# Attention of a two-layer trunk on one core: both heads of a pair in one operation for small blocks, fillers accumulated in the scores' PSUM banks, a shorter scale chain and another order of fillers

## The chip, the cores and the metric

The kernel runs on one core of a Trainium2 chip. The metric is device time in microseconds, as the median of several executions. Five engines run side by side, each through its own instructions in order: PE multiplies matrices (its weight loads are listed as PEld), DVE and ACT work element by element, POOL does small jobs and some DMA issues, SP issues the weight DMAs. Matrix products end in PSUM, which has eight banks of 128 x 512 float32 here; ACT and DVE carry results from there to on-chip memory.

## The reference

One sequence of 512 tokens of width 1024 goes through two layers. Layer 0 is attention and a gated MLP, layer 1 a gated short convolution and another MLP. All is float32. The attention has 8 forgetting heads (softmax) and 8 stick-breaking heads; cut to what matters here:

```python
q_fox = rms_norm(q[:, :H_FOX], fox_q_g)          # the same for k, and for the stick-breaking heads
logits = einsum('bhqd,bhkd->bhqk', qi, k) * scale + fi[..., :, None] - cum_f[:, :, None, :]
p = softmax(where(causal, logits, -inf));  o_fox = p @ v

z = einsum('bhqd,bhkd->bhqk', qi, k) * scale                     # stick breaking
log_one_minus = where(strict, log_sigmoid(-z), 0.0)
later = cumsum(log_one_minus, reverse=True) - log_one_minus
w = where(strict, exp(log_sigmoid(z) + later), 0.0);  o_sb = w @ v
out = concatenate([o_fox, o_sb]) @ w_out
```

## The kernel before

Every large product is done as three matmuls on a high and a low part of each operand (`mm3`, lines 248 to 250, and `mm3_rhs`, 503 to 505), to keep float32 accuracy. Weights come by DMA in tiles `raw` and are split by ACT (line 227, `whi`) and DVE (line 228, `wlo`).

The attention works on pairs of heads p = 0 to 7 (0 to 3 forgetting, 4 to 7 stick-breaking) and query blocks b = 0 to 3 of 128 rows; a block (p, b) has n = 128(b+1) keys. For a block, `logits` puts the scores of the two heads e = 0, 1 into two PSUM banks, and ACT and DVE turn them into weights `w`: maximum, exponential, reciprocal and scaling for forgetting heads; two sigmoids, a backward scan (line 639) and a product (line 640) for the others. `turn` transposes `w` on PE into a bank `psc` and splits the result into `pt` (ACT line 662, DVE line 663). `weigh` multiplies two blocks' `pt` with the values into a bank `psa`, and ACT and DVE (lines 688, 689) read it out as `o`.

Between those steps PE gets other work, "fillers": generators that yield after each step of a product. `queries_keys(p)` makes the queries and keys of a pair, with their sums of squares (`sums`, line 539), a transpose of these (`turned_sums`, 547), a reciprocal root on DVE (`scales`, lines 549 to 568) and transposes of the widened scale (`rows`, line 575); `values(g)` makes the values of two pairs; `output(0)` is the first half of the output projection. `fill(us)` spends a quota of filler work by a running clock of estimated PE time, `after(us, fn)` puts a function on that clock. The constants at the head set those quotas and delays: `PRE` is the filler work ahead of the first block, `ROWS` the delay from the scale chain to the transposes of `rows`.

PSUM is dealt out by `bank(tag)`: two banks "a" (queries, keys, values, `weigh`, output), four banks "b" (scores) and two banks "c" (all transposes and small sums). The program is written in this order, but a scheduler then sets each engine's order, by its own costs and by which slots are free; the excerpts of that order below show the result. Names there carry numbers: `psa168_2985` is one allocation of a bank "a", `w420` the weights of pair 4, block 2, head 0, `qk_hi60` the high part of the queries of pair 6, and a bracket tells which engines' semaphores the instruction waits for.

Of the kernel before, what the change touches and what calls it, by code (L numbers as in the profile page):

```python
# [25 lines left out]
P = 128  # L26
S = 512
# [23 lines left out]
def trunk(  # L51
# [207 lines left out]
    class Norm:  # L259
# [23 lines left out]
                dve.tensor_tensor(self.acc, self.acc, sq, op=ALU.add)  # L283

        def scale(self, sums):
            v = tiny.tile([P, NB], F32, tag="nv", name=f"nv_{self.name}")
# [195 lines left out]
    def values(g):  # L482
        ws = [weights(), weights(AHEAD - 1)]
        v = v_tiles[g] = ap_.tile([P, NB, 4, 2, HD], F32R, tag="v", name=f"v{g}", bufs=2)
        n = 256 if g else 264
        for b in range(NB):
            acc = bank("a")
            tok = slice(b * P, (b + 1) * P)
            for k in range(ND):
                w = ws[k // 4]  # L490
                mm3_rhs(acc[:, 0:n], (hs_hi[:, k, tok], hs_lo[:, k, tok]), (w[0][:, k % 4, :], w[1][:, k % 4, :]), k == 0, k == ND - 1)
                spend(0.33)
                yield 1
# [3 lines left out]
            dve.scalar_tensor_tensor(v[:, b, :, 1, :], src, r, f32(v[:, b, :, 0, :]), op0=ALU.mult, op1=ALU.subtract)  # L497
# [6 lines left out]
        pe.matmul(acc, lhs[0], w[1], start=False, stop=False)  # L504
        pe.matmul(acc, lhs[1], w[0], start=False, stop=last)  # L505

    rx2 = const.tile([P, NB], F32, tag="rx2", name="rx2")

    def square_norm():
        dve.tensor_tensor(rx2, norm.col, norm.col, op=ALU.mult)  # L510
        dve.tensor_scalar(rx2, rx2, 1.0 / HD, None, op0=ALU.mult)

    halves, q_scale, done = {}, {}, set()

# [5 lines left out]
    def queries_keys(p):  # L520


        fox = p < 4
        v = tiny.tile([P, NB, 2, 2], F32, tag="qv", name=f"qv{p}")
        r = tiny.tile([P, NB, 2, 2], F32, tag="qr", name=f"qr{p}")
        kept, got, sqs = {}, {}, []
        halves[p] = got

# [16 lines left out]
        def turned_sums(t, flat):  # L545
            for i in range(2):
                pe.transpose(t[:, (2 + i) * P:(3 + i) * P], flat[:, i * P:(i + 1) * P], ident)
            spend(0.25)
            dve.tensor_tensor(
                v, t[:, 2 * P:4 * P].rearrange("p (i b c) -> p b i c", i=2, b=NB)[:, :, :, 0:2],  # L550
                rx2[:, :, None, None].to_broadcast([P, NB, 2, 2]), op=ALU.mult,
            )
            scales()

        def scales():
            vf, rf = (t.rearrange("p b i h -> p (b i h)") for t in (v, r))
            dve.tensor_scalar(vf, vf, EPS, None, op0=ALU.add)
            rsqrt(rf, vf, 16, f"qk{p}")
            rf = r.rearrange("p b i h -> p b (i h)")
            dve.tensor_tensor(rf, rf, norm.col[:, :, None].to_broadcast([P, NB, 4]), op=ALU.mult)  # L560
            if not fox:
                s = q_scale[p] = aw.tile([P, 2, NB, 2], F32, tag="qscale", name=f"qscale{p}", bufs=3)
                dve.tensor_copy(s[:, 0], r[:, :, 1, :])
                dve.tensor_scalar(s[:, 1], r[:, :, 1, :], -1.0, None, op0=ALU.mult)
            wides = {}
            for i in kept:
                wides[i] = work.tile([P, S], F32, tag="u0", name=f"qwide{p}{i}").rearrange("p (b h d) -> p b h d", b=NB, h=2)
                dve.tensor_copy(wides[i], r[:, :, i, :][:, :, :, None].to_broadcast([P, NB, 2, HD]))
            after(ROWS, lambda: rows(wides))

        def rows(wides):
# [7 lines left out]
            done.add(("qk", p))  # L579

        for i in range(2):
            acc = bank("a")
            yield from products(acc, weights())
            sq = work.tile([P, S], F32, tag="sq", name=f"sq_{p}{i}")
            act.activation(sq, acc, AF.Square)
# [7 lines left out]
                act.activation(kept[i], acc, AF.Copy, scale=g)  # L593
            sqs.append(sq)
        after(SUMS, sums)

    def logits(p, b):

# [19 lines left out]
        ws = []  # L618
        for e in range(2):
            s = ss[e]  # L620
            w = aw.tile([P, S], F32, tag="w", name=f"w{p}{b}{e}", bufs=WB)
            ws.append(w)
            if fox:
                top = tiny.tile([P, 1], F32, tag="top", name=f"top{p}{b}{e}")
                dve.reduce_max(top, s[:, 0:n], axis=AX.X, negate=True)
                total = tiny.tile([P, 1], F32, tag="total", name=f"total{p}{b}{e}")
                act.activation(w[:, 0:n], s[:, 0:n], AF.Exp, bias=top, accum_out=total)
                inv = tiny.tile([P, 1], F32, tag="inv", name=f"inv{p}{b}{e}")
                dve.reciprocal(inv, total)
                dve.tensor_scalar(w[:, 0:n], w[:, 0:n], inv, None, op0=ALU.mult)  # L630
            else:
                scale = q_scale[p]
                rest = aw.tile([P, S], F32, tag="rest", name=f"rest{p}{b}{e}")
                act.activation(rest[:, 0:n], s[:, 0:n], AF.Sigmoid, scale=scale[:, 1, b, e:e + 1])
                act.activation(w[:, 0:n - 1], s[:, 0:n - 1], AF.Sigmoid, scale=scale[:, 0, b, e:e + 1])

                pool.memset(w[:, n - 1:n], 0.0)
                back = rest[:, 1:n][:, ::-1]
                dve.tensor_tensor_scan(back, back, begin[:, S - n + 1:S][:, ::-1], 0.0, op0=ALU.mult, op1=ALU.max)  # L639
                dve.tensor_tensor(w[:, 0:n - 1], w[:, 0:n - 1], rest[:, 1:n], op=ALU.mult)  # L640
        return ws

    pts = {}

    def turn(p, b, ws):

        half, n = b // 2, (b + 1) * P
        if b % 2 == 0:
            pts[p, half] = []
            for e in range(2):  # L650
                both = [aw.tile([P, NB, 256], F32R, tag=f"pt{i}", name=f"pt{p}{half}{e}{i}", bufs=PT) for i in range(2)]
                for t in both:
                    pool.memset(f32(t[:, 2 * half + 1, 0:P]), 0.0)
                pts[p, half].append(both)
        at_ = slice((b % 2) * P, (b % 2 + 1) * P)
        for e in range(2):
            t = bank("c")
            for k in range(b + 1):
                pe.transpose(t[:, k * P:(k + 1) * P], ws[e][:, k * P:(k + 1) * P], ident)  # L659
            src = t[:, 0:n].rearrange("p (k q) -> p k q", q=P)  # L660
            hi, lo = pts[p, half][e]
            act.activation(hi[:, 0:b + 1, at_], src, AF.Copy)
            dve.tensor_tensor(lo[:, 0:b + 1, at_], src, f32(hi[:, 0:b + 1, at_]), op=ALU.subtract)
        spend(0.22 * (b + 1))

    def weigh(p, half):
# [5 lines left out]
        to = slice(half * 256, (half + 1) * 256)  # L672
        last = 2 * half + 1
        for e in range(2):
            hi, lo = pts[p, half][e]
            for k in range(last + 1):
                w = v[:, k, 2 * (p % 2) + e].rearrange("p i d -> p (i d)")
                pe.matmul(acc[:, e * 256:(e + 1) * 256], w, hi[:, k, :], start=k == 0, stop=False)
                pe.matmul(acc[:, e * 256:(e + 1) * 256], w, lo[:, k, :], start=False, stop=k == last)
# [131 lines left out]
    after(NORM0, lambda: (norm.scale(sums0), square_norm()))  # L811
    for k in range(ND):
        next(qk0)
    flush()
# [1 line left out]
    attn = ExitStack()  # L816
    ap_ = attn.enter_context(tc.tile_pool(name="attn", bufs=1))
    aw = attn.enter_context(tc.tile_pool(name="aw", bufs=2))

# [9 lines left out]
    run(values(0))  # L829
    log_gate()  # L830
    load_gains()
    for g, ps_ in enumerate(((1, 2), (3, 4), (5, 6), (7,))):
        fillers.extend(queries_keys(p) for p in ps_)
        if g < 3:
            fillers.append(values(g + 1))
# [177 lines left out]
```

## Time and profile before

| what | before |
| --- | --- |
| median of 3 runs | 1221.25 us (1220.8 to 1221.3) |
| profiled execution | 1220.77 us, span 1219.0 us |
| PE busy | 1204.0 us, 99% of the span, 5841 instructions |
| DVE busy | 762.8 us, 63% |
| ACT busy | 503.4 us, 41% |
| POOL busy | 26.6 us, 2% |
| mean busy share of the DMA engines, 40 to 260 us | 0.20 |

The span runs from the first to the last instruction; the profiled execution is 1.8 us longer than its span. The attention lies between about 23 and 260 us of the span; ahead of it are the first norm and products, behind it the output projection's end, the MLPs and the convolution.

### The profile page before, as it was taken

The page shows a single profiled execution, that of the slowest core. Times are in us where ns is not written, and L with a number is a line of the kernel's source. Part 1 is how long each engine was busy: PE and PEld are TensorE (multiplying, and loading weights), DVE is VectorE, ACT ScalarE, POOL GpSimd, SP SyncE. Part 2 cuts the span into 40 slices and gives each one's busy share as a digit, 9 for nine tenths or more (in the row PEclk, how much of TensorE's full clock was granted, in tenths as well). Part 3 has the DMA queues.
Part 4 walks back from the last instruction along what each step waited for, and adds up shares of the span by engine and source line. Part 5 has one row for each costly group of instructions (what it writes and reads, how often), then busy time and mean ns, then how long its engine had stood idle before and what let it go on. Part 6 is the DMA issues. An engine that isn't in the chain of part 4 may idle for free.

```text
span 1219.0 us, 15006 instructions
## 1 busy us (share of the span) xinstructions
PE 1204.0 (99%) x5841; PEld 973.4 (80%) x5841; DVE 762.8 (63%) x1250; ACT 503.4 (41%) x787; POOL 26.6 (2%) x139
## 2 busy tenths in 40 slices
PE   8999999999999999999999999999999999999998
PEld 7887877778888888888888888888888888888886
DVE  5887888887867777663333555465776767672222
ACT  6556576655544443432222222233434344442120
POOL 4000000000000000000000000000000000000000
PEclk9999999999999999999999999999999999999999
DMA  7312121213233333323333333323233332322330
GB/s 196 88 36 70 36 69 36 70 62 96 87 102 89 97 93 94 96 81 93 94 95 104 89 102 87 104 87 104 87 93 98 89 102 87 103 87 88 121 102 35
DMA packets 182696, 108.14 MB, mean 89 GB/s; under 512 B 4732, under 2 KB 175020, under 8 KB 182624
## 3 DMA queue, kind: packets, MB, share of 16 engines
q1 hardware_dynamic: 182080, 106.94, 29.7%
q8 instruction: 46, 0.75, 0.3%
q0 software_dynamic: 384, 0.17, 0.1%
q14 instruction: 26, 0.21, 0.1%
q10 hardware_dynamic: 160, 0.07, 0.0%
HBM read 105.06 MB, written 2.10 MB: 88 GB/s over the span
## 4 chain that ended last, share of the span: by engine, by line
PE 91%; DVE 6%; ACT 2%; issue 1%; DMA 0%; SPq 0%; DVEq 0%; POOL 0%; ACTq 0%
PE psa L248 13%; PE psa L250 12%; PE psa L249 12%; PE psb L248 12%; PE psb L250 12%; PE psb L249 12%; PE psa L503 2%; PE psa L504 2%; PE psa L505 2%; PE psb L504 2%; PE psb L503 2%; PE psb L505 2%; DVE rest L639 1%; PE psc L659 1%; PE psb L610 1%
## 5 line engine op out<-in xcount | busy, mean ns | idle before, releaser
L227 ACT ACTIVATE whi<-raw 128x1024 fp32r<-128x1024 f32 (+3 forms) x199 | 208.9, 1050 | 362.7 <-PE psb L249 134.9
L228 DVE TENSOR_TENSOR wlo<-raw,whi 128x1024 fp32r<-128x1024 f32 (+3 forms) x199 | 240.4, 1209 | 160.2 <-ACT whi L227 159.1
L248 PE MATMUL psa<-hs_hi,whi 128*128 128x512 f32 x544 | 219.4, 403 | 2.5 <-DVE o L689 1.3
L250 PE MATMUL psa<-hs_hi,wlo 128*128 128x512 f32 x544 | 215.1, 395 | 0.2 <-DVE wlo L228 0.2
L249 PE MATMUL psa<-hs_lo,whi 128*128 128x512 f32 x544 | 214.6, 395 | 0.0
L248 PE MATMUL psb<-hs_hi,whi 128*128 128x512 f32 x480 | 189.9, 396 | 0.0
L250 PE MATMUL psb<-hs_hi,wlo 128*128 128x512 f32 x480 | 189.8, 395 | 0.0
L249 PE MATMUL psb<-hs_lo,whi 128*128 128x512 f32 x480 | 188.7, 393 | 0.0
L347 DVE SCALAR_TENSOR_TENSOR u<-y,taps,u 128x510 f32<-128x510 f32 (+1 forms) x176 | 131.1, 748 | 3.3 <-ACT u L344 0.4
L248 PEld LDWEIGHTS psa<-hs_hi,whi 128*128 128x128 f32 x544 | 102.3, 188 | 25.7 <-issue 2.3
L250 PEld LDWEIGHTS psa<-hs_hi,wlo 128*128 128x128 f32 x544 | 102.2, 188 | 25.0 <-DVE wlo L228 1.1
L249 PEld LDWEIGHTS psa<-hs_lo,whi 128*128 128x128 f32 x544 | 102.3, 188 | 22.2 <-DVE hs_lo L758 0.4
L249 PEld LDWEIGHTS psb<-hs_lo,whi 128*128 128x128 f32 x480 | 90.1, 188 | 21.4
L250 PEld LDWEIGHTS psb<-hs_hi,wlo 128*128 128x128 f32 x480 | 90.1, 188 | 21.4
L248 PEld LDWEIGHTS psb<-hs_hi,whi 128*128 128x128 f32 x480 | 90.3, 188 | 20.2
L885 DVE TENSOR_TENSOR y<-psb,nrow_n 128x512 f32<-128x512 f32 x44 | 30.4, 691 | 83.3 <-PE psb L250 83.3
L339 ACT ACTIVATE a<-u 128x512 fp32r<-128x512 f32 x44 | 27.9, 634 | 118.7 <-DVE u L890 118.7
L889 ACT ACTIVATE u<-u 128x512 f32<-128x512 f32 x44 | 27.9, 633 | 91.3 <-DVE u L347 91.3
L344 ACT ACTIVATE u<-y,taps 128x512 f32<-128x512 f32 x88 | 63.1, 719 | 1.2 <-DVE y L885 1.1
L340 DVE TENSOR_TENSOR a<-u,a 128x512 fp32r<-128x512 f32 x44 | 30.5, 692 | 29.4 <-ACT a L339 29.4
L503 PE MATMUL psa<-whi,hs_hi 128*128 128x256 f32 (+1 forms) x128 | 38.3, 299 | 0.8 <-ACT qk L593 0.7
L505 PE MATMUL psa<-whi,hs_lo 128*128 128x256 f32 (+1 forms) x128 | 36.3, 283 | 0.0
(251 smaller groups left out, 1818.3 us busy)
## 6 DMA issues: line engine op xcount, KB each, us to landing
raw<-in_ffn_w_up SPq DMA_DIRECT2D x88, 512.0 KB, 3.8
raw<-in_ffn_w_down SPq DMA_DIRECT2D x30, 512.0 KB, 3.7
raw<-in_attn_w_in SPq DMA_DIRECT2D x24, 512.0 KB, 4.0
raw<-in_conv_w_in SPq DMA_DIRECT2D x24, 512.0 KB, 3.8
raw<-in_ffn_w_down SPq DMA_DIRECT2D x16, 448.0 KB, 3.6
raw<-in_attn_w_out SPq DMA_DIRECT2D x8, 512.0 KB, 3.5
raw<-in_conv_w_out SPq DMA_DIRECT2D x8, 512.0 KB, 3.9
x_tok<-in_x SPq DMA_DIRECT2D x4, 512.0 KB, 6.5
```

The source lines that it names most:

```text
L227: return (act.activation(hi[:, at_], raw[:, at_], AF.Copy), dve.tensor_tensor(lo[:, at_], raw[:, at_], f32(hi[:, at_]), op=ALU.subtract))
L228: dve.tensor_tensor(lo[:, at_], raw[:, at_], f32(hi[:, at_]), op=ALU.subtract))
L248: made = [pe.matmul(acc, w[0], rhs[0], start=first, stop=False), pe.matmul(acc, w[0], rhs[1], start=False, stop=False), pe.matmul(acc, w[1 ...
L249: pe.matmul(acc, w[0], rhs[1], start=False, stop=False),
L250: pe.matmul(acc, w[1], rhs[0], start=False, stop=last)]
L340: dve.tensor_tensor(lo, src, f32(hi), op=ALU.subtract)
L344: act.activation(dst, src, AF.Copy, scale=tap(2))
L347: dve.scalar_tensor_tensor(dst[:, d:], src[:, 0:S - d], tap(j), dst[:, d:], op0=ALU.mult, op1=ALU.add)
L503: pe.matmul(acc, lhs[0], w[0], start=first, stop=False)
L504: pe.matmul(acc, lhs[0], w[1], start=False, stop=False)
L505: pe.matmul(acc, lhs[1], w[0], start=False, stop=last)
L885: dve.tensor_tensor(y, acc, norm.row, op=ALU.mult)
```

## The change

- In `logits` and `turn`, blocks with b < 2 are done for both heads at once (`at_once`): one reciprocal, one product with the scanned row, one PSUM bank of transposes and one split into `pt`, where two stood before. Blocks with b = 2, 3 keep one operation per head. `w` and `pt` become one tile for both heads, with the same total of buffers.
- The scanned row `rest` is one tile for the whole attention, placed at its right end, with a column of zeros behind it; the memsets of the last column of `w` on POOL go.
- `queries_keys` for p >= 1 and `values` for g >= 1 accumulate in banks "b" in place of "a".
- The scale chain: `least`, made once, and one operation on DVE (scale and add) stand for a product, an addition and a later product with `ncol` for each pair.
- Fillers run in the order 1, 2, v1, 3, 4, 5, v2, 6, 7, v3 in place of 1, 2, v1, 3, 4, v2, 5, 6, v3, 7. `PRE` goes from 12 to 14, `ROWS` from 5 to 8.

```diff
-PRE = 12.0
+PRE = 14.0
-SUMS, FLAT, ROWS = 3.0, 1.5, 5.0
+SUMS, FLAT, ROWS = 3.0, 1.5, 8.0
...
-    for g, ps_ in enumerate(((1, 2), (3, 4), (5, 6), (7,))):
+    for g, ps_ in enumerate(((1, 2), (3, 4, 5), (6, 7), ())):
...
     def values(g):
...
-            acc = bank("a")
+            acc = bank("b" if g >= 1 else "a")
...
-            dve.tensor_tensor(
-                v, t[:, 2 * P:4 * P].rearrange("p (i b c) -> p b i c", i=2, b=NB)[:, :, :, 0:2],
-                rx2[:, :, None, None].to_broadcast([P, NB, 2, 2]), op=ALU.mult,
+            dve.scalar_tensor_tensor(
+                v.rearrange("p i b h -> p (i b) h"), t[:, 2 * P:4 * P].rearrange("p (j c) -> p j c", c=32)[:, :, 0:2],
+                1.0 / HD, least[:, :, None].to_broadcast([P, 2 * NB, 2]), op0=ALU.mult, op1=ALU.add,
             )
...
-            dve.tensor_scalar(vf, vf, EPS, None, op0=ALU.add)
             rsqrt(rf, vf, 16, f"qk{p}")
-            dve.tensor_tensor(rf, rf, norm.col[:, :, None].to_broadcast([P, NB, 4]), op=ALU.mult)
...
-            acc = bank("a")          # in queries_keys
+            acc = bank("b" if p >= 1 else "a")
...
+    def at_once(b):
+        return (slice(0, 2),) if b < 2 else (slice(0, 1), slice(1, 2))
...
+            for es in at_once(b):
+                for e in range(es.start, es.stop):
+                    act.activation(rest[:, e, keys], ss[e][:, 0:n], AF.Sigmoid, scale=scale[:, 1, b, e:e + 1])
+                    act.activation(w[:, e, :], ss[e][:, 0:n], AF.Sigmoid, scale=scale[:, 0, b, e:e + 1])
+                    back = rest[:, e, keys][:, ::-1]
+                    dve.tensor_tensor_scan(back, back, begin[:, keys][:, ::-1], 0.0, op0=ALU.mult, op1=ALU.max)
+                dve.tensor_tensor(w[:, es], w[:, es], rest[:, es, S - n + 1:S + 1], op=ALU.mult)
...
-        for e in range(2):
-            t = bank("c")
-            for k in range(b + 1):
-                pe.transpose(t[:, k * P:(k + 1) * P], ws[e][:, k * P:(k + 1) * P], ident)
-            src = t[:, 0:n].rearrange("p (k q) -> p k q", q=P)
-            hi, lo = pts[p, half][e]
-            act.activation(hi[:, 0:b + 1, at_], src, AF.Copy)
-            dve.tensor_tensor(lo[:, 0:b + 1, at_], src, f32(hi[:, 0:b + 1, at_]), op=ALU.subtract)
+        for es in at_once(b):
+            t = bank("c")[:, 0:(es.stop - es.start) * n].rearrange("p (e k q) -> p e k q", k=b + 1, q=P)
+            for e in range(es.start, es.stop):
+                for k in range(b + 1):
+                    pe.transpose(t[:, e - es.start, k, :], w[:, e, k * P:(k + 1) * P], ident)
+            act.activation(hi[:, es], t, AF.Copy)
+            dve.tensor_tensor(lo[:, es], t, f32(hi[:, es]), op=ALU.subtract)
```

What stands where moves on every engine. On PE, where the scores of block (6, 0) are made (`psb` with queries `qk_hi60`), and a filler's product begins in a bank "a" in their midst; before:

```order
L610 MATMUL psb169_3004<-qk_hi60_2889,qk_hi61_2657 128x256 [waits Activation_49]
L248 MATMUL psa168_2985<-hs_hi_111,whi22_2662 128x512 [waits DVE_49,PE_49]
L249 MATMUL psa168_2985<-hs_lo_112,whi22_2662 128x512
L250 MATMUL psa168_2985<-hs_hi_111,wlo22_2663 128x512
L248 MATMUL psa168_2985<-hs_hi_111,whi22_2662 128x512
L249 MATMUL psa168_2985<-hs_lo_112,whi22_2662 128x512
L250 MATMUL psa168_2985<-hs_hi_111,wlo22_2663 128x512
L610 MATMUL psb170_3005<-qk_hi60_2889,qk_hi61_2657 128x256
L610 MATMUL psb169_3004<-qk_lo60_2890,qk_hi61_2657 128x256
```

The same block after; the filler is now `values(3)`, already under way in a bank "b", and the transposes of `w53` stand between the scores' first and later parts:

```order
L504 MATMUL psb154_2737<-wlo23_2629,hs_hi_111 128x256
L612 MATMUL psb155_2750<-qk_hi60_2714,qk_hi61_2477 128x256 [waits Activation_49]
L612 MATMUL psb156_2751<-qk_hi60_2714,qk_hi61_2477 128x256
L505 MATMUL psb154_2737<-whi23_2628,hs_lo_112 128x256
L657 MATMUL psc157_2775<-ident_84,w53_2663 128x128 [waits DVE_49]
L657 MATMUL psc157_2775<-ident_84,w53_2663 128x128 x3
L657 MATMUL psc158_2782<-ident_84,w53_2663 128x128 [waits DVE_49]
L657 MATMUL psc158_2782<-ident_84,w53_2663 128x128 x3
L612 MATMUL psb155_2750<-qk_lo60_2715,qk_hi61_2477 128x256 [waits DVE_49]
```

The first filler matmul no longer asks for a bank "a"; the scores themselves still wait for the queries that ACT and DVE split.

On PE, the transposes of block (4, 2), whose first head goes to one bank "c" and whose second to the other; before, the sums of pair 5 (`flat5`) hold a bank too:

```order
L659 MATMUL psc140_2516<-ident_84,w420_2397 128x128 x2
L547 MATMUL psc138_2479<-ident_84,flat5_2488 128x128 [waits Activation_49]
L547 MATMUL psc138_2479<-ident_84,flat5_2488 128x128
L248 MATMUL psa135_2438<-hs_hi_111,whi18_2236 128x512
L249 MATMUL psa135_2438<-hs_lo_112,whi18_2236 128x512
L250 MATMUL psa135_2438<-hs_hi_111,wlo18_2237 128x512
L248 MATMUL psa135_2438<-hs_hi_111,whi18_2236 128x512
L249 MATMUL psa135_2438<-hs_lo_112,whi18_2236 128x512
L250 MATMUL psa135_2438<-hs_hi_111,wlo18_2237 128x512
L659 MATMUL psc141_2522<-ident_84,w421_2404 128x128 [waits DVE_49]
```

and after:

```order
L675 MATMUL psa131_2390<-pt401_2271,v2_1999 128x256
L657 MATMUL psc132_2412<-ident_84,w42_2322 128x128 x3
L657 MATMUL psc133_2418<-ident_84,w42_2322 128x128 [waits PE_49]
L657 MATMUL psc133_2418<-ident_84,w42_2322 128x128 x2
L248 MATMUL psb130_2380<-hs_hi_111,whi19_2300 128x512
```

The pair's sums have moved to another place, and the second head's transposes follow the first's without a wait for DVE.

On DVE, the blocks (4, 0) and (4, 1); before, scan and product are four operations for a block, and the split of the transposes two:

```order
L639 SCALAR_TENSOR_TENSOR rest410_2310<-rest410_2310,begin_89 128x255 [waits Activation_49]
L663 TENSOR_TENSOR pt3111_2197<-psc124_2282,pt3110_2196 128x4x128 [waits Activation_49]
L640 TENSOR_TENSOR w410_2309<-w410_2309,rest410_2310 128x255 [waits DVE_49,Activation_49]
L228 TENSOR_TENSOR wlo19_2330<-raw19_2328,whi19_2329 128x1024 [waits DMAHW2_49,PE_49,Activation_49]
L639 SCALAR_TENSOR_TENSOR rest411_2317<-rest411_2317,begin_89 128x255 [waits Activation_49]
L640 TENSOR_TENSOR w411_2316<-w411_2316,rest411_2317 128x255 [waits DVE_49,Activation_49]
L663 TENSOR_TENSOR pt4001_2362<-psc129_2369,pt4000_2361 128x128 [waits PE_49,Activation_49,Pool_49]
L663 TENSOR_TENSOR pt4011_2366<-psc130_2373,pt4010_2365 128x128 [waits PE_49,Activation_49,Pool_49]
```

and after:

```order
L639 SCALAR_TENSOR_TENSOR rest_357<-rest_357,begin_89 128x256 [waits Activation_49] x2
L640 TENSOR_TENSOR w41_2212<-w41_2212,rest_357 128x2x256 [waits DVE_49,Activation_49]
L497 SCALAR_TENSOR_TENSOR v2_1999<-psb117_2182,ncol_n0_324,v2_1999 128x4x64 [waits Activation_49]
L575 TENSOR_TENSOR qn50_2257<-qk50_1912,psc122_2252 128x512 [waits PE_49]
L685 TENSOR_TENSOR o31_2263<-psa121_2235,o31_2263 64x256 [waits Activation_49]
L659 TENSOR_TENSOR pt401_2271<-psc123_2274,pt400_2270 128x2x128 [waits Activation_49,Pool_49]
```

The product and the split stand once for both heads.

More of the change, by code (lines that the diff above doesn't have):

```diff
@@ L285, in scale @@
         def scale(self, sums):
[L286 removed]
+            v = self.mean = tiny.tile([P, NB], F32, tag="nv", name=f"nv_{self.name}")
             dve.tensor_scalar(v, sums, 1.0 / D, EPS, op0=ALU.mult, op1=ALU.add)
@@ L505, in mm3_rhs, with least_square @@
         pe.matmul(acc, lhs[1], w[0], start=False, stop=last)
[L507 to L511, printed above, removed]
+    least = const.tile([P, 2 * NB], F32, tag="least", name="least")
+    def least_square():
+        for i in range(2):
+            dve.tensor_scalar(least[:, i * NB:(i + 1) * NB], norm.mean, EPS, None, op0=ALU.mult)
     halves, q_scale, done = {}, {}, set()
@@ L523, in queries_keys @@
         fox = p < 4
-        v = tiny.tile([P, NB, 2, 2], F32, tag="qv", name=f"qv{p}")
-        r = tiny.tile([P, NB, 2, 2], F32, tag="qr", name=f"qr{p}")
+        v = tiny.tile([P, 2, NB, 2], F32, tag="qv", name=f"qv{p}")
+        r = tiny.tile([P, 2, NB, 2], F32, tag="qr", name=f"qr{p}")
         kept, got, sqs = {}, {}, []
@@ L617, in logits @@
         spend((4 if fox else 3) * wide * 0.00044 + (0.12 if fox else 0))
-        ws = []
-        for e in range(2):
[L620 to L640, printed above, removed]
@@ L641, in logits @@
-        return ws
+        w = aw.tile([P, 2, S], F32, tag="w", name=f"w{p}{b}", bufs=2)[:, :, 0:n]
+        if fox:
+            top, total, inv = (tiny.tile([P, 2], F32, tag=t, name=f"{t}{p}{b}") for t in ("top", "total", "inv"))
+            for e in range(2):
+                dve.reduce_max(top[:, e:e + 1], ss[e][:, 0:n], axis=AX.X, negate=True)
+                act.activation(w[:, e, :], ss[e][:, 0:n], AF.Exp, bias=top[:, e:e + 1], accum_out=total[:, e:e + 1])
+            for es in at_once(b):
+                dve.reciprocal(inv[:, es], total[:, es])
+                for e in range(es.start, es.stop):
+                    dve.tensor_scalar(w[:, e, :], w[:, e, :], inv[:, e:e + 1], None, op0=ALU.mult)
+        else:
+            scale = q_scale[p]
+            keys = slice(S - n, S)
+            for es in at_once(b):
[5 more added lines that the diff above has]
+                dve.tensor_tensor(w[:, es], w[:, es], rest[:, es, S - n + 1:S + 1], op=ALU.mult)
@@ L674, in weigh @@
         for e in range(2):
-            hi, lo = pts[p, half][e]
+            hi, lo = (t[:, e] for t in pts[p, half])
             for k in range(last + 1):
@@ L810, in trunk @@
         after(b + 0.5, lambda b=b: squares(b))
-    after(NORM0, lambda: (norm.scale(sums0), square_norm()))
+    after(NORM0, lambda: (norm.scale(sums0), least_square()))
     for k in range(ND):
@@ L818, in trunk @@
     aw = attn.enter_context(tc.tile_pool(name="aw", bufs=2))
+    rest = aw.tile([P, 2, S + 1], F32, tag="rest", name="rest", bufs=1)
+    pool.memset(rest[:, :, S:S + 1], 0.0)
     o_tiles = {0: mixed(0)}
@@ L831, in trunk @@
     load_gains()
-    for g, ps_ in enumerate(((1, 2), (3, 4), (5, 6), (7,))):
+    for g, ps_ in enumerate(((1, 2), (3, 4, 5), (6, 7), ())):
         fillers.extend(queries_keys(p) for p in ps_)
```

26 lines of the change are left out of this document (12 added, 14 removed).

## The prediction

> **What bounds the kernel.** I read the page first, then the busy time by stretch, then the list of who waited for whom on PE.
>
> ```profile
> span 1219.0 us, 15006 instructions
> ...
> PE 1204.0 (99%) x5841; PEld 973.4 (80%) x5841; DVE 762.8 (63%) x1250; ACT 503.4 (41%) x787; POOL 26.6 (2%) x139
> ```
>
> PE is busy all but 15.0 us of the span. By stretch (after the length come PE, PEld, DVE, ACT and POOL busy, the granted clock and the DMA share):
>
> ```profile
> 0.00:23.00 23.00, 20.12 (x124) 15.77 (x124) 13.28 (x20) 17.02 (x28) 12.24 (x46) 1.00 0.73 206
> 23.00:40.00 17.00, 16.59 (x133) 15.35 (x131) 12.58 (x51) 8.64 (x16) 0.53 (x1) 1.00 0.37 99
> 40.00:260.00 220.00, 212.10 (x1426) 169.68 (x1425) 181.69 (x461) 136.68 (x310) 13.05 (x88) 1.00 0.20 59
> 260.00:1219.00 959.00, 955.20 (x4165) 772.57 (x4163) 555.30 (x721) 341.11 (x436) 0.76 (x5) 1.00 0.31 93
> ```
>
> The change touches the stretch from 40 to 260. There PE sits idle 220.00 - 212.10 = 7.9 us, at clock 1.00, with DMA at 0.20, and DVE is busy 83% of it. So the ceiling is low: this is a change for those 7.9 us and little else. PE's waits (total, times, longest):
>
> ```profile
> PE psc L659 <- DVE pt L663: 1.7, 2, 1.4
> PE psa L248 <- DVE o L689: 1.6, 2, 1.3
> PE psc L575 <- DVE pt L663: 1.4, 2, 0.9
> PE psa L248 <- DVE h L727: 1.3, 1, 1.3
> ...
> PE psa L503 <- ACT qk L593: 0.7, 2, 0.4
> PE psc L539 <- ACT sq L585: 0.5, 1, 0.5
> ...
> PE psc L575 <- DVE qwide L568: 0.5, 1, 0.5
> PE psc L539 <- DVE pt L663: 0.3, 1, 0.3
> ...
> PE psa L678 <- DVE v L497: 0.2, 1, 0.2
> ```
>
> Most wait for a bank: `psc` until DVE has split an older transpose into `pt`, or `psa` until `o` or `qk` is read out. Not one is for `w` (the softmax or the scan) or for a score bank `psb`. Two places, in time (start, length):
>
> ```profile
> 178.36 0.40 PE L249 MATMUL psa<-hs_lo,whi 128*128 128x512 f32 x1
> 178.59 0.39 PE L250 MATMUL psa<-hs_hi,wlo 128*128 128x512 f32 x1
> 180.36 0.55 PE L659 MATMUL psc<-ident,w 128*128 128x128 f32 x3 [1.38 <-DVE pt L663]
> ```
>
> and on DVE at that time:
>
> ```profile
> 176.90 0.69 DVE L640 TENSOR_TENSOR w<-w,rest 128x511 f32<-128x511 f32 x1
> 177.51 1.22 DVE L639 TENSOR_TENSOR_SCAN rest<-rest,begin 128x511 f32<-128x511 f32 x1
> 178.82 0.69 DVE L640 TENSOR_TENSOR w<-w,rest 128x511 f32<-128x511 f32 x1
> 179.43 0.41 DVE L689 TENSOR_TENSOR o<-psa,o 64x256 f32<-64x256 f32 x1
> 179.77 0.54 DVE L663 TENSOR_TENSOR pt<-psc,pt 128x384 fp32r<-128x384 f32 x1
> ```
>
> This is the wait of `w421` in the order above. The split of the first head's transposes stands on DVE behind a scan, a product and `o`, and ends at 180.31; PE starts at 180.36. Two matmuls start 0.23 us apart but count as busy for 0.39, so each listed wait hides 0.16 us more: this one costs 180.36 - 178.82 = 1.54, not 1.38.
>
> ```profile
> 211.00 0.38 PE L610 MATMUL psb<-qk_hi,qk_hi 64*128 64x256 f32 x1
> 212.69 0.47 PE L248 MATMUL psa<-hs_hi,whi 128*128 128x512 f32 x1 [1.32 <-DVE o L689]
> ```
>
> This is `psa168` of the order: a new filler product needs a bank "a" that `weigh` has just filled and DVE not yet read.
>
> **The change, part by part.** PE has as many instructions after as before, 5833 in the order; nothing is taken from PE but waits and turns.
>
> Banks "a". Fillers for p, g >= 1 leave them, so the wait at 212.69 (1.3) goes, and the smaller of the two `qk` waits (0.7 - 0.4 = 0.3; the other is at the first pair, which stays in "a"). With 0.16 each: -1.9 us. The waits for `h` (1.3) and for `o` at the output projection (0.3) stay; that filler is still in "a".
>
> Banks "c". Five waits, 1.7 + 1.4 + 0.3 = 3.4, with the hidden part 4.2. I laid PE's order end to end (0.23 us for 512 columns, in proportion below, 0.12 for a transpose: an estimate) and counted the allocations that follow within 3.0 us of PE time on the last write of the tile that must come free; the split at 179.77 came free 3 us after its transposes. In "c" there were 24 of these in the attention and are 11, since small blocks take one bank instead of two. I take the waits in proportion, 11/24 kept: -2.3. Ends: 0, if the 11 are the ones that bite, and -4.2.
>
> `rows`. Three more units of `ROWS` put the widened scale's transposes behind the scale chain: the 0.5 (0.7 in full) for `qwide` goes. -0.7; ends 0 and -0.7.
>
> Turns of PE. Scores use half the rows of the array. The order holds them in 38 unbroken runs before and in 34 after (the first excerpt is one of the broken ones).
>
> ```profile
> 205.26 0.28 PE L505 MATMUL psa<-whi,hs_lo 128*128 128x256 f32 x1
> 205.47 0.50 PE L610 MATMUL psb<-qk_hi,qk_hi 64*128 64x512 f32 x2
> ...
> 206.36 0.39 PE L503 MATMUL psa<-whi,hs_hi 128*128 128x256 f32 x1
> ```
>
> From 205.26 to 206.36 is 1.10 us; a 256-wide matmul and three pairs of 512 take 0.12 + 3 x 0.23 = 0.81 without turns. So entering and leaving costs 0.28 us, and four runs fewer -1.1; ends 0 and -1.6.
>
> DVE. Sixteen splits of 128 columns become eight of 256, sixteen of 256 eight of 512, and the scale chain loses two operations of eight pairs:
>
> ```profile
> L663 DVE TENSOR_TENSOR pt<-psc,pt 128x512 fp32r<-128x512 f32 x16 | 10.6, 686 | 1.4 <-ACT pt L662 1.3
> ...
> L663 DVE TENSOR_TENSOR pt<-psc,pt 128x256 fp32r<-128x256 f32 x16 | 6.3, 416 | 0.9 <-ACT pt L662 0.8
> ...
> L663 DVE TENSOR_TENSOR pt<-psc,pt 128x128 fp32r<-128x128 f32 x16 | 4.4, 286 | 3.8 <-ACT pt L662 1.6 <-POOL pt L653 1.3 <-POOL w L637 0.8
> ...
> L557 DVE TENSOR_SCALAR qv<-qv 128x16 f32<-128x16 f32 x8 | 1.4, 172 | 0.2
> ```
>
> 16 x 0.286 - 8 x 0.416 = 1.2; 16 x 0.416 - 8 x 0.686 = 1.2; 16 x 0.172 = 2.8: 5.2 us less of 181.7. DVE is off PE's path, so I book nothing for it; what it does is shorten the queue in which `pt` and `o` stand. The joined reciprocals and products, ACT's joined copies and POOL's memsets likewise: no PE wait names them.
>
> What is added. The scores of (6, 0) stand, by the same laying out, 1.8 us behind the transposes of `qwide60`, and their queries must go through a product, ACT's split and DVE's on a full DVE. Before, pairs 3, 5 and 7 stood as near (1.7 us) and the list has no wait for them: 0 at best, and at worst 1.4, the longest wait that a full DVE made. +0.7. In banks "b" three allocations fall within 3.0 us where none did: +0.3; ends 0 and 1.4. `PRE` only moves filler work forward; PE does the same sum of it. The joined blocks need both heads' weights at their first transpose: the order leaves (0, 0) 3.1 us and the others 4.8 us or more, and before (0, 0) had 2.5 without a wait: 0.
>
> Sum: -1.9 - 2.3 - 0.7 - 1.1 + 0.7 + 0.3 = -5.0. The span goes from 1219.0 to 1214.0, the profiled execution from 1220.77 to 1215.8. The median lies 0.5 above that execution, 1221.25, so 1216.2; I say 1216.
>
> **The rivals.** *All of it goes* (0.26). A DVE with a shorter queue also ends the waits for `h`, `sq` and `v` and those left in "c". Then 7.9 of idle time goes with 12 x 0.16 = 1.9 hidden and 1.1 of turns, and half of the added 1.0 stays: -10.4, 1211. For it speaks that in all banks together the near allocations fall from 42 to 19; against it that DVE stays at 80% and keeps its 1.22 us scans.
>
> *The waits move* (0.16). DVE still serves `pt`, `o`, `qn` and the weights' `wlo` in one queue; if a wait is DVE's backlog whatever the bank, PE meets it at the next bank. Only turns and one `psa` wait are gained, -1.1 - 1.5 + 1.0: 1219.7. For it speaks that both places above end on DVE.
>
> *The score banks run short, slower* (0.07). 26 filler products now each hold one of four banks "b" for some 5 us, and the scores of a block need two at once, so a block's scores can wait for the block before to be read by ACT. The order leaves 4.3 us or more for that in most of the 32 blocks; if ACT reads later than that, each wait takes PE with it, fillers and all. At 0.4 us in 24 blocks, 9.6 us less the 5.0: 1226. It decides at about 13 such waits. Against it: no `psb` wait now. [...] The first three rows of waits bear out that it is banks PE waits for; the spacing in the order says they rotate further apart after.
>
> **How the numbers follow.** My forecast holds 0.51. A median that differs by less than 0.2% (2.4 us, above 1218.8) can't be told from no change. The forecast and the first rival lie below that: faster 0.77; the second is the same, 0.16; the last slower, 0.07. The range, 1210.5 to 1220.0, takes in the first three.
>
> **What would show it.** In the changed kernel, PE idle from 40 to 260 us of about 4 us in place of 7.9; no wait of a `psb` filler or of `psa` ahead of the output projection; `psc` waits of some 1.6 in all; the `qwide` wait gone; at most a small wait on the scores at (6, 0); DVE busy about 176 us there. I am wrong if waits named `psb` appear by the dozen, or if PE's idle time stays at 7.

## The result and the profile after

The changed kernel takes 1212.38 us (median of 6 runs, 1212.25 to 1212.49) against 1221.28 beside it: 8.9 us less, a ratio of 0.9928 with a 95% interval of 0.9915 to 0.9940. The profiled execution took 1212.38 us. Its page begins:

```profile
span 1210.5 us, 14824 instructions
...
PE 1200.0 (99%) x5841; PEld 974.7 (81%) x5841; DVE 755.6 (62%) x1202; ACT 501.3 (41%) x771; POOL 21.5 (2%) x76
```

PE's idle time fell by 4.5 us (15.0 to 10.5), its busy time by 4.0 with the same 5841 matmuls. A matmul's row lasts longer than the distance to the next one (0.39 against 0.23 us for 512 columns), so part of each wait and all of a turn stand in the "busy" number. By stretch (columns as before):

```profile
0.00:23.00 23.00, 20.81 (x116) 16.64 (x116) 12.63 (x20) 16.32 (x26) 12.23 (x45) 1.00 0.71 199
23.00:40.00 17.00, 16.61 (x135) 15.40 (x136) 11.91 (x50) 9.21 (x16) 0.00 (x0) 1.00 0.42 109
40.00:260.00 220.00, 215.94 (x1477) 176.83 (x1476) 184.79 (x429) 140.81 (x307) 9.28 (x31) 1.00 0.21 61
260.00:1210.50 950.50, 946.67 (x4119) 765.86 (x4117) 546.31 (x707) 334.96 (x425) 0.00 (x0) 1.00 0.31 93
```

From 40 to 260 PE idles 4.06 us where it idled 7.90, and gets through 1477 instructions where it got through 1426. All of PE's waits over the whole span:

```profile
PE psa L248 <- DVE o L685: 1.4, 1, 1.4
PE psc L728 <- DVE blank L77: 1.0, 1, 1.0
PE psc L573 <- DVE pt L659: 1.0, 1, 1.0
PE psa L248 <- DVE h L723: 0.8, 1, 0.8
PE psc L657 <- DVE pt L659: 0.7, 2, 0.4
PE psa L248 <- ACT whi L227: 0.5, 1, 0.5
PE psc L540 <- DVE head_gains L152: 0.5, 1, 0.5
PE psa L503 <- ACT qk L591: 0.2, 1, 0.2
PE psa L250 <- DVE wlo L228: 0.2, 1, 0.2
```

No row names a `psb` filler, `qwide`, `sq` or `v`. The place of the 1.32 us wait at 212.69, the scores of (6, 0), now reads (PE, start and length):

```profile
205.75 0.39 PE L612 MATMUL psb<-qk_hi,qk_hi 64*128 64x256 f32 x2
206.06 0.39 PE L505 MATMUL psb<-whi,hs_lo 128*128 128x256 f32 x1
...
207.47 0.28 PE L612 MATMUL psb<-qk_hi,qk_lo 64*128 64x256 f32 x2
207.69 0.39 PE L503 MATMUL psb<-whi,hs_hi 128*128 128x256 f32 x1
```

The first scores are followed by a filler product in a "b" bank after 0.31 us and the last by another after 0.22 us, neither with a wait. The longest wait that is left stands at the output projection, on PE and then on DVE:

```profile
254.63 0.40 PE L249 MATMUL psb<-o_lo,whi 128*128 128x512 f32 x1
256.46 0.47 PE L248 MATMUL psa<-o_hi,whi 128*128 128x512 f32 x1 [1.43 <-DVE o L685]
```

```profile
251.12 1.22 DVE L639 TENSOR_TENSOR_SCAN rest<-rest,begin 128x512 f32<-128x512 f32 x1
252.44 0.69 DVE L640 TENSOR_TENSOR w<-w,rest 128x512 f32<-128x512 f32 x1
253.05 1.22 DVE L639 TENSOR_TENSOR_SCAN rest<-rest,begin 128x512 f32<-128x512 f32 x1
254.37 0.69 DVE L640 TENSOR_TENSOR w<-w,rest 128x512 f32<-128x512 f32 x1
254.98 0.41 DVE L685 TENSOR_TENSOR o<-psa,o 64x256 f32<-64x256 f32 x1
...
255.88 0.43 DVE L685 TENSOR_TENSOR o<-psa,o 64x256 f32<-64x256 f32 x1
```

It is the picture of the kernel before at 180 us: the readout of `o` stands on DVE behind two scans and two products, and the product that wants the bank waits for it.

For all kernels below I also took, for every two PE instructions in a row between 20 and 300 us, the time between their starts less what that form of matmul needs (the fastest tenth of its kind: 0.23 us for 512 columns). The sum is the **lost time** of the attention, hidden parts included (good to some 0.5 us, by how the fastest tenth is taken): 73.0 us before, 64.8 after, -8.2. The waits in it went from 11.1 to 4.9.

A fixed stretch of the clock holds more of the program once the kernel is faster, so I also took the time between the same two matmuls, the first of `sums` (`psc<-sq,head_ones`) and the last of the output projection (the last `psa<-o_hi,wlo`). They start at 22.62 and 292.20 us before, at 23.16 and 283.68 after. That is 269.58 and 260.52 us: the attention gives 9.06 us. What stands behind takes 926.8 us in both. The head gives nothing: idle time in the first 23 us fell from 2.88 to 2.19 us, but `sums` begins 0.54 us later, as PE gets through 116 instructions there in place of 124. So 9.06 - 0.54 = 8.5 us is the difference of the two spans; the profiled execution of the kernel before lies 0.5 us under its median, which makes it 8.9. The start of `sums` varies from 22.62 to 23.95 us over the profiled executions of all kernels but e13, which gives `sums` another place.

### The profile page after: what moved, and what is told of

Read it like the earlier page. It is cut to its first block, busy times and chain, and to the rows that moved or that the text cites. A ratio compares the mean times of both kernels' runs of the same rounds, so it can differ in the third digit from the quotient of the medians.

```text
span 1210.5 us, 14824 instructions
## 1 busy us (share of the span) xinstructions
PE 1200.0 (99%) x5841; PEld 974.7 (81%) x5841; DVE 755.6 (62%) x1202; ACT 501.3 (41%) x771; POOL 21.5 (2%) x76
## 4 chain that ended last, share of the span: by engine, by line
PE 94%; DVE 3%; ACT 2%; issue 0%; DVEq 0%; ACTq 0%
PE psb L248 14%; PE psb L250 14%; PE psb L249 14%; PE psa L248 11%; PE psa L250 11%; PE psa L249 11%; PE psb L503 2%; PE psb L504 2%; PE psb L505 2%; PE psa L503 2%; PE psa L504 2%; PE psa L505 2%; PE psb L612 1%; PE psc L657 1%; PE psa L674 1%; PE psa L675 1%
## 5 line engine op out<-in xcount | busy, mean ns | idle before, releaser
L248 PE MATMUL psb<-hs_hi,whi 128*128 128x512 f32 x592 | 237.7, 401 | 0.0
L250 PE MATMUL psb<-hs_hi,wlo 128*128 128x512 f32 x592 | 234.0, 395 | 0.0
L249 PE MATMUL psb<-hs_lo,whi 128*128 128x512 f32 x592 | 232.7, 393 | 0.0
L248 PE MATMUL psa<-hs_hi,whi 128*128 128x512 f32 x432 | 171.5, 397 | 0.5 <-ACT whi L227 0.5
L250 PE MATMUL psa<-hs_hi,wlo 128*128 128x512 f32 x432 | 170.8, 395 | 0.3 <-DVE wlo L228 0.2
L249 PE MATMUL psa<-hs_lo,whi 128*128 128x512 f32 x432 | 170.5, 395 | 0.0
L250 PEld LDWEIGHTS psb<-hs_hi,wlo 128*128 128x128 f32 x592 | 111.2, 188 | 26.4
L249 PEld LDWEIGHTS psa<-hs_lo,whi 128*128 128x128 f32 x432 | 81.1, 188 | 19.3 <-DVE hs_lo L754 0.4
L503 PE MATMUL psa<-whi,a 128*128 128x512 f32 x88 | 35.5, 403 | 0.0
L503 PE MATMUL psb<-whi,a 128*128 128x512 f32 x88 | 34.9, 396 | 0.0
```

Source lines behind the costliest of these rows:

```text
L248: made = [pe.matmul(acc, w[0], rhs[0], start=first, stop=False), pe.matmul(acc, w[0], rhs[1], start=False, stop=False), pe.matmul(acc, w[1 ...
L249: pe.matmul(acc, w[0], rhs[1], start=False, stop=False),
L250: pe.matmul(acc, w[1], rhs[0], start=False, stop=last)]
L503: pe.matmul(acc, lhs[0], w[0], start=first, stop=False)
```

## The experiments

Twelve kernels ran, all timed beside the kernel before. "Near" counts the allocations within 3.0 us of the last write of their bank's former tile, laid out as in the prediction but from 25 to 265 us, so that the counts of before and after read 46 and 21 instead of 42 and 19.

| kernel | us | ratio (95%) | lost time 20 to 300 | waits in it | near a, b, c |
|---|---|---|---|---|---|
| before | 1221.2 | 1 | 73.0 | 11.1 | 20, 0, 26 |
| changed | 1212.4 | 0.9928 (0.9915 to 0.9940) | 64.8 | 4.9 | 7, 3, 11 |
| e1: before, banks | 1216.8 | 0.9963 (0.9950 to 0.9975) | 69.1 | 7.8 | 7, 5, 21 |
| e2: changed, old banks | 1219.7 | 0.9988 (0.9979 to 0.9997) | 71.3 | 10.6 | 20, 1, 13 |
| e9: before, joined blocks | 1220.6 | 0.9993 (0.9984 to 1.0002) | 72.6 | 10.5 | 21, 0, 16 |
| e7: changed, old chain | 1213.3 | 0.9936 (0.9924 to 0.9949) | 65.3 | 5.1 | 7, 3, 11 |
| e3: changed, blocks not joined | 1212.5 | 0.9929 (0.9917 to 0.9942) | 64.9 | 5.0 | 7, 3, 21 |
| e4: changed, old filler order | 1213.9 | 0.9941 (0.9929 to 0.9954) | 65.2 | 5.0 | 8, 3, 11 |
| e5: changed, ROWS 5 | 1216.5 | 0.9959 (0.9946 to 0.9973) | 68.7 | 8.3 | 7, 1, 12 |
| e6: changed, PRE 12 | 1215.5 | 0.9951 (0.9939 to 0.9964) | 67.9 | 7.1 | 4, 2, 13 |
| e11: before, banks and numbers | 1212.4 | 0.9930 (0.9918 to 0.9943) | 65.4 | 5.1 | 7, 3, 21 |
| e12: before, no scans | 1217.8 | 0.9972 (0.9962 to 0.9982) | 70.0 | 8.0 | 19, 0, 28 |
| e8: changed, output(0) in "b" | 1210.1 | 0.9911 (0.9898 to 0.9925) | 62.5 | 2.7 | 2, 3, 11 |
| e13: e8, `sums` in "a" | 1208.6 | 0.9899 (0.9886 to 0.9913) | 61.8 | 1.9 | 3, 3, 6 |

An interval is some 1.5 us to each side, so by the intervals e3, e4, e7, e11 and e8 can't be told from the changed kernel. The executions are closer together than that: 1212.25 to 1212.49 for the changed kernel, 1213.30 to 1215.19 for e4, 1210.01 to 1210.93 for e8.

**Banks alone, and all but banks.** The theory: the distance between two uses of a bank makes the gain. The rival: DVE's shorter queue.

```diff
 # e1, to the kernel before (e2 takes the same two lines back in the changed kernel)
-            acc = bank("a")            # values(g)
+            acc = bank("b" if g >= 1 else "a")
-            acc = bank("a")            # queries_keys(p)
+            acc = bank("b" if p >= 1 else "a")
```

> The kernel before with one part of the change: products of queries, keys and values go to banks "b" from the second pair on. The theory (what counts is how far a bank's next use stands from its last): the near allocations of "a" fall from 20 to 7 as in the full change, those of "c" stay (26 to 21, 14 of them closer than 2 us before and now). So the 1.7 of the `o` wait at 212.69 and 0.3 of `qk` go, and 38 unbroken runs of scores become 35, 0.8: about -2.8, 1218.5 us. The rival (DVE's queue sets it, whatever the bank): DVE has all its operations, so the waits move to the next bank and only the turns are gained: 1220.5 us.

> The changed kernel with those products back in banks "a", all else changed. The theory: 20 near allocations of "a" as before, so the `o` wait of 1.7 and the `qk` wait of 0.3 are back, and 37 runs of scores instead of 34 cost 0.8: 1212.4 + 2.8 = 1215.2 us, with a `psa` wait on `o` of over 1 us between 180 and 230 us. The rival: DVE is as light as in the full change, so hardly a wait returns: 1212.4 to 1213.2 us.

e1: 1216.8 us, -4.5, where the theory gave -2.8 and the rival 1220.5 us. The `o` wait at 212.69 is gone, and of the waits that the theory had left in place `sq` and `v` are too. e2: 1219.7, +7.3 where the theory gave +2.8. The banks "a" bring back not one wait but a family: on `h` 1.77 with the hidden part (1.08 in the changed kernel), on `v` 1.02, on `o` 0.69, 0.62 and 0.54, on `qk` 0.72, and a `psc` wait of 1.62 at 207. The rival has fallen twice: e1 gains with all of DVE's operations, and with DVE as light as in the changed kernel e2 has 10.6 us of waits. What these two don't separate is whether it helps more that the fillers leave the banks of `weigh`, or that they get four banks to take turns in.

**Joined blocks and the shorter chain.** e9 takes the joined blocks alone (`at_once`, `turn`, the tiles `w`, `rest` and `pt`). Its expectation names the shorter scale chain too, but the kernel that ran keeps the old one: its DVE still has the 16 operations that the chain would save (`qv<-qv` x8, 1.4 us, and `qr<-qr,ncol_n` x8, 1.4 us). So DVE is 2.4 us lighter in e9 and not 5.2. e7 puts the old chain back into the changed kernel.

> The kernel before with the joined blocks and the shorter scale chain alone; banks, PRE, ROWS and the order of fillers as before. The theory: near allocations of "c" fall from 26 to 16 (14 to 9 closer than 2 us), those of "a" stay at 21: a good third of the 4.2 us of "c" waits goes, -1.6: 1219.7 us; the `psa` waits on `o` and `h` of over 1 us stay. The rival: DVE is 5.2 us lighter, which is all that the queue needs: most of the 8.9 us is there already, 1214 us.

> The changed kernel with the old scale chain: two more operations on DVE for each of eight pairs, 2.8 us of DVE between 15 and 190 us; PE's order is the same to the instruction. The theory: DVE is off PE's path, and `rows` stand 8 units behind the chain: 1212.4 to 1212.9 us. The rival: DVE's load makes the waits, and 2.8 of the 5.2 us of relief are taken back, so half of what it had brought: 1215 us or more.

e9: 1220.6, an interval that holds no change, and 10.5 us of waits. "c" had 16 near allocations instead of 26 for it: the count went down and the time did not. The rival's case, a DVE lighter by all 5.2 us with nothing else changed, did not run; e2, which has both parts, stands against it. e7 has the changed kernel's PE order with 2.8 us more on DVE: 1213.3, between the theory's 1212.9 and the rival's 1215, and hardly told from 1212.4; the same five waits, `o` at 256 being 1.97 instead of 1.60. Its executions with a mean clock of 1.000 took 1212.56 to 1213.31, the two at 0.999 took 1214.16 and 1214.27, so part of the 0.9 may be the clock (see the last section).

```diff
 # e3, to the changed kernel
-        return (slice(0, 2),) if b < 2 else (slice(0, 1), slice(1, 2))
+        return (slice(0, 1), slice(1, 2))
```

> The changed kernel with the heads of every block apart (two banks "c" for each block, also for b = 0 and 1); banks "b", chain, PRE, ROWS and order as changed. What is open is where the 4.4 us between the banks alone (1216.8) and the full change (1212.4) come from. The theory (distance of banks): near allocations of "c" go from 11 back to 21, the number that the banks-only kernel has, and that kernel's `psc` waits on `pt` sum to 3.8 us with the hidden part against 2.2 in the changed one: +1.6, and DVE's 2.4 us more count for nothing: 1214.0 us. The rival (ROWS, PRE and order of the fillers make the rest): 1212.4 to 1213 us.

1212.5: the theory's +1.6 did not come. PE's waits from 20 to 300 us in e3:

```profile
PE psa L248 <- DVE o L685: 1.4, 1, 1.4
PE psc L573 <- DVE pt L659: 1.0, 1, 1.0
PE psc L657 <- DVE qn L575: 1.0, 1, 1.0
PE psc L657 <- DVE pt L659: 0.7, 2, 0.4
```

The `pt` waits are those of the changed kernel, though "c" has ten more near allocations; one of 1.0 on `qn` has come and the one on `h` is gone. So the joined blocks did not shorten the `psc` waits.

**The numbers.** e4, e5 and e6 each put one back: the order ((1, 2), (3, 4), (5, 6), (7,)), ROWS = 5, PRE = 12.

> The changed kernel with the old order of fillers, ((1, 2), (3, 4), (5, 6), (7,)) with values between. Near allocations stay (8, 3 and 11 in "a", "b", "c", against 7, 3 and 11) and the scores stand in 35 unbroken runs instead of 34. The theory (distance of banks and turns): 1212.4 to 1213.0 us. The rival (the order makes a large part of the 4.4 us that the banks alone don't bring): 1214 us or more.

> The changed kernel with ROWS = 5 instead of 8: the transposes of the widened scale stand 3 units closer behind the scale chain. Near allocations of "c" 12 instead of 11, nine instead of six of them closer than 2 us. The theory: a wait on `qwide` of about 0.6 is back, 0.5 more in "c": 1213.2 us, with a `qwide` wait in the list. The rival (the transposes wait for banks, not for the scale, so ROWS is worth nothing): 1212.4 us and no `qwide` wait.

> The changed kernel with PRE = 12 instead of 14: two units less filler work ahead of the first block. Near allocations 4, 2 and 13 in "a", "b", "c" against 7, 3 and 11. The theory (PRE only moves filler work): 1212.0 to 1212.8 us. The rival (the work ahead of the first block keeps the fillers ahead of all later needs): waits on the scores or on `qk` appear, 1214 us or more.

All three have about as few near allocations as the changed kernel. e4's waits sum to the same 5.0, but they are others: `o` and `h` are gone, and one of 2.07 has come. Its profiled execution is 1.8 us longer in the span than the changed kernel's; 0.8 of that lies ahead of the first `sums` (23.95 us against 23.16) and 0.9 in the attention. Its median of 1213.9 falls between its theory (1213.0) and its rival (1214). e5 and e6 are slower by 4.1 and 3.1. For e5 that is past both its theory and its rival, and it has no `qwide` wait at all. For e6 the rival (1214 us or more) came out in the number; of the waits on the scores that it named there is one, 0.4 us on `qk_hi`, and the rest is `pt`. In e5 PE and DVE show this:

```profile
228.81 0.39 PE L612 MATMUL psb<-qk_hi,qk_hi 64*128 64x256 f32 x2
231.61 0.80 PE L248 MATMUL psa<-o_hi,whi 128*128 128x512 f32 x1 [2.42 <-DVE h L723]
232.20 0.63 PE L249 MATMUL psa<-o_lo,whi 128*128 128x512 f32 x1
232.63 0.63 PE L250 MATMUL psa<-o_hi,wlo 128*128 128x512 f32 x1
...
234.63 0.39 PE L249 MATMUL psa<-o_lo,whi 128*128 128x512 f32 x1
234.86 0.39 PE L250 MATMUL psa<-o_hi,wlo 128*128 128x512 f32 x1
```

```profile
227.82 1.22 DVE L639 TENSOR_TENSOR_SCAN rest<-rest,begin 128x512 f32<-128x512 f32 x1
229.15 0.69 DVE L640 TENSOR_TENSOR w<-w,rest 128x512 f32<-128x512 f32 x1
229.75 1.22 DVE L639 TENSOR_TENSOR_SCAN rest<-rest,begin 128x512 f32<-128x512 f32 x1
230.89 0.67 DVE L723 TENSOR_TENSOR h<-psa,h 128x512 f32<-128x512 f32 x1
```

The readout of `h` that the product waits for stands behind two scans and a product, and the wait is 2.42 us where the changed kernel has 0.84. Then PE ran slowly: 0.43 us from one matmul to the next instead of 0.23. By stretches, of e5 and then of e6, which has a wait of 2.54 that ends at 202.47 (the granted clock is the third number from the end):

```profile
227.62:231.03 3.41, 1.57 (x14) 1.20 (x12) 3.31 (x5) 1.78 (x4) 0.56 (x2) 1.00 0.73 258
231.03:234.45 3.42, 2.84 (x7) 2.29 (x8) 3.23 (x7) 0.79 (x2) 0.00 (x0) 0.50 0.11 43
234.45:237.86 3.41, 3.41 (x21) 2.55 (x20) 1.71 (x2) 2.11 (x6) 0.00 (x0) 1.00 0.00 0
```

```profile
200.44:203.85 3.41, 1.38 (x8) 1.24 (x9) 3.25 (x8) 0.80 (x2) 0.00 (x0) 1.00 0.02 5
203.85:207.26 3.41, 3.41 (x11) 2.16 (x11) 1.52 (x3) 1.69 (x2) 0.00 (x0) 0.50 0.00 0
```

The clock is at half for 3.4 us in both. In e5 it falls 0.6 us before PE's restart, so 2.8 us of work pay for it; in e6 it falls 1.4 us after the restart, and all of the 3.4 us do. Of e5's five executions, the one with a mean clock of 1.000 took 1214.78 and the others, at 0.998 to 0.999, 1216.34 to 1216.85; e6's took 1214.21 and 1214.28 against 1215.49 to 1216.09. So ROWS = 5 costs 2.4 us as waits, by that one execution, and some 1.7 more in the executions with a lower mean clock. e4's hole, with the matmul behind it, kept the clock at 1.00 in the profiled execution:

```profile
228.23 0.48 PE L248 MATMUL psa<-o_hi,whi 128*128 128x512 f32 x1
230.78 0.55 PE L657 MATMUL psc<-ident,w 128*128 128x128 f32 x3 [2.07 <-DVE qv L550]
231.08 0.48 PE L249 MATMUL psa<-o_lo,whi 128*128 128x512 f32 x1
```

e11 puts banks and the three numbers into the kernel before, and leaves the rewritten blocks and the chain out.

> The kernel before with banks "b" and the three edits of numbers (PRE 14, ROWS 8, the new order of fillers); blocks not joined, old scale chain. Near allocations 7, 3 and 21 in "a", "b", "c". The theory now (banks and where the fillers stand make the change; the joined blocks are worth 0.1 and the chain 0.9, as their undoing showed): 1212.4 + 1.0 = 1213.4 us. The rival (the rewritten blocks are needed to keep "c" free, and their undoing cost nothing only because the shorter chain stood by): 1215 us or more.

1212.4, the time of the whole change, with lost time of 65.4 against 64.8. Two lines of banks and three edits of numbers make the change; the rewriting of the blocks and the chain adds nothing that shows here. e9 had said so of the blocks from the other side. Banks and numbers need each other: the numbers bring 4.4 us beside the new banks (e1 against e11), but all that e2 has besides the banks brings 1.5 us. Nor do the numbers add up: undone one at a time they cost 1.5 + 4.1 + 3.1 = 8.7 us, and all three together bring 4.4.

**What makes a near allocation bite.** e12 leaves the backward scans out of the kernel before, so that its weights are products of unscanned sigmoids.

```diff
-                back = rest[:, 1:n][:, ::-1]
-                dve.tensor_tensor_scan(back, back, begin[:, S - n + 1:S][:, ::-1], 0.0, op0=ALU.mult, op1=ALU.max)
```

> The kernel before without the backward scans of the stick-breaking heads (32 pairs of blocks; the weights are then products of the unscanned sigmoids, so the output differs). DVE has 25.9 us less to do from 145 us on; banks, order of the fillers and near allocations (19, 0, 28) as before. The theory (a near allocation bites only where DVE has a queue of scans and products ahead of the readout): the six longest waits after 145 us, 1.69 + 1.54 + 1.52 + 1.09 + 0.63 + 0.59 = 7.1 us with the hidden part, fall to a third, 1216.5 us. The rival (the distance between a bank's uses decides by itself): waits as before, 1220.5 us or more.

1217.8 us, between the two. PE's order moved at a few places only. Its waits from 20 to 300 us begin:

```profile
PE psc L575 <- DVE pt L661: 1.4, 2, 0.9
PE psc L575 <- DVE qwide L568: 0.9, 3, 0.5
PE psa L248 <- DVE o L687: 0.8, 2, 0.5
```

Of the three long waits, `o` at 212 went from 1.69 to 0.79, `pt` at 180 from 1.54 and `h` at 237 from 1.52 to below 0.3 us. The three of 1.09, 0.63 and 0.59 stayed (1.08, 0.62 and 0.58). So a near allocation that makes a wait costs 0.6 to 1.1 us here without the scans; with them in the queue three of these waits had 1.5 to 1.7 in this kernel, and e5 and e6 have waits of up to 2.8 with the hidden part. Both theories held a part. Which of the 46 near allocations make one of the dozen or so waits is not shown.

**Aiming at the waits that are left.** e8 and e13 go after the rows by name:

```diff
 # e8: output(g, done)
-            acc = bank("a")
+            acc = bank("b")
 # e13: the same, and in sums() of queries_keys
-            t = bank("c")
+            t = bank("a")
```

> The changed kernel with the accumulators of the first half of the output projection in banks "b" too, so that "a" is left to `weigh` and the first pair. Near allocations of "a" fall from 7 to 2, the others stay at 3 and 11. The theory: the waits for `o` (1.60 at 256.46) and `h` (1.08 at 228.75) go: 1209.7 us. The rival (PE meets DVE's backlog at the next place, as single numbers showed when they moved a wait of 1 to 3 us from one bank to another): 1211.5 to 1213 us.

> The kernel of e8_out_b with the banks of `sums` moved from "c" to "a" as well, which now has room. Near allocations 3, 3 and 6 in "a", "b", "c", 12 in all against 21 in the changed kernel and 46 before. The theory: besides the 2.7 us of `o` and `h`, about half of the 2.25 us of `psc` waits on `pt` goes: 1208.6 us. The rival (the backlog is met at the next place): 1211.5 to 1213 us.

1210.1 and 1208.6 us, 0.4 above and 0.05 below the theory's numbers; the rivals' 1211.5 to 1213 did not come. The intervals of the two overlap, and so do those of e8 and the changed kernel; the waits (4.9, 2.7 and 1.9 us) go the same way as the times. The waits of over 0.2 us from 20 to 300 us, of e8 and then of e13:

```profile
PE psc L657 <- DVE pt L659: 1.0, 3, 0.4
PE psc L573 <- DVE pt L659: 0.9, 1, 0.9
PE psc L540 <- DVE head_gains L152: 0.5, 1, 0.5
```

```profile
PE psc L573 <- DVE pt L659: 0.9, 1, 0.9
PE psc L142 <- DVE h L761: 0.4, 1, 0.4
PE psc L657 <- DVE pt L659: 0.3, 1, 0.3
```

No `psa` wait on `o` or `h` in either. e13 is the fastest kernel here: 12.7 us below the kernel before, 3.8 below the changed one, with 1.38 us of idle time left from 40 to 260 us. Its profiled execution is the slowest of four (1209.96; the others 1208.02 to 1208.59), with a mean clock of 0.999 where the others have 1.000.

## Why the prediction was right, and where its sum was not

The direction, the mechanism (waits for banks) and nearly every row that it named came out: idle time about 4 us from 40 to 260 (4.06), no `psb` wait, no `psa` wait between 40 us and the output projection, `psc` waits of 1.6 (1.7), no `qwide` wait, none at (6, 0). The size was short, -5.2 against -8.9; the time lies nearer to the first rival's 1211 than to 1216. That rival's reason, a DVE with a shorter queue, is not borne out: e11 reaches the same time with all of DVE's operations. By the terms of the sum:

- Banks "a", -1.9. The waits named there went as forecast. But the banks alone bring 4.5 us (e1), and the kernel without them (e2) is 7.3 us slower: the term is by far the largest. I had priced it only by the two rows that stood in the list, while e2 has six of 0.5 to 1.0 us on `o`, `qk` and `v` ahead of the output projection. `sq` (0.79) and `v` (0.33) are gone in e1 already.
- Banks "c", -2.3, by the share of near allocations. The size was right: the `psc` waits on `pt` are 4.4 us before and 2.25 after with their hidden parts. The cause was wrong, so the size was luck. The joined blocks, for which I booked it, are worth nothing that shows (e3, e9, e11); with the banks alone these waits are 3.8 us, and with banks and numbers 2.35 (e11). This is the step that failed, and with it the counting: e5 and e6 have 20 and 19 near allocations and are slower than the changed kernel with 21, e3 and e11 have 31 and are not.
- `rows`, -0.7. The `qwide` wait is gone, yet with ROWS = 5 it does not come back; what comes is 1.7 us more on the `h` bank, a new wait of 1.4 for a bank "c", and the lower clock. That the 0.7 fits the row was luck too. "`PRE` only moves filler work forward" booked at nothing what e6 measures as 3.1 us beside the other two numbers (before them it was not measured). In a list of waits a number of the schedule has no row of its own, and I took its one visible wait for its whole price.
- Turns, -1.1. Between the two matmuls above, entering and leaving the runs of scores cost 9.4 us of lost time before and 8.0 after, -1.4: about right.
- DVE, 0. e7's 0.9 us for half of that relief is within what can't be told apart, so that 0 is not refuted. That DVE would be busy 176 us from 40 to 260 was wrong (184.79): over the whole span it fell by 7.2, but PE no longer idled there and so pulled 51 more of its own instructions, with their readouts, into that stretch.
- Added, +1.0: nothing of it came. The scores of (6, 0) and the fillers in "b" do not wait.
- Kept, `h` 1.3 and `o` 0.3 at the output projection: 0.84 and 1.43. The second grew, which is the rival *The waits move* on a small scale.

So of the 9.1 us in the attention some 6 are waits, where I had added up 3.9; 1.4 are turns, where I had 1.1; and the rest, more than 1.5 us, is many small gaps between matmuls, for which I had nothing. *The score banks run short* did not happen: "b" has three near allocations, none of which waits.

## What to carry to other kernels

When a full engine reads out the banks of a busy one, look for the bank that two kinds of work share at short distance and move one of them to the bank group whose rows show no wait; then go on by the name of each wait that is left, which gave times within 0.4 us of the forecast, twice. A count of close allocations forecast little here, and operations saved on the reading engine brought nothing that showed. Before crediting rewritten code, put the bank and number edits that came with it into the old kernel without it, as e11 does; undoing one number at a time tells which ones matter, but the costs do not add up.

## What the runs showed of the hardware

Around the end of a hole of 2.42 us (e5) and of one of 2.54 us (e6) in PE's work the granted clock was 0.50 for 3.4 us, and matmuls stood 0.43 us apart instead of 0.23, a rate of 0.23 / 0.43 = 0.54. PE was idle for 1.84 of the 3.41 us ahead of the fall in e5, and for 2.03 in e6. The other twelve profiled executions have a granted clock of 1.00 from 40 to 260 us, e4 with its hole of 2.07 us among them (PE idle for 2.07 of the 4.00 us from 228 to 232).

Which holes cost the clock is not shown beyond that. The executions of one kernel differ by their mean clock: four of e5's five have 0.998 or 0.999 and one has 1.000, three of e6's five 0.998 or 0.999 and two 1.000, two of e7's five 0.999 and three 1.000. There is one trace for each kernel, so it is not shown whether a stretch at 0.50, as in the traces of e5 and e6, stands behind the lower means of the executions without one.
